# The fourth feed-forward's gate and upper half: seven half-size products in place of eight for sixteen of its 22 column tiles

## The chip, the cores and the metric

The kernel runs on one core of a Trainium2 chip. The metric is the device time of one launch in microseconds; the median of three timed runs is compared. A second kind of run is profiled: one execution of the program recorded by the hardware profiler, from which all rows below come.

## The reference

The model is a two-layer backbone with four feed-forward blocks (FFNs). The change concerns the last of them. All tensors are float32; there are 512 tokens, the model width is 1024 and the hidden width `D_FF` is 2816.

```
def swiglu(h, w_gu, w_down):
    g, u = jnp.split(h @ w_gu, 2, axis=-1)
    return (jax.nn.silu(g) * u) @ w_down
...
x = x + 0.5 * m[8] * swiglu(modulate(x, m[6], m[7]), ffn_w_gu[l, 1], ffn_w_down[l, 1])
```

`modulate` is an RMS norm with a scale and a shift. Behind the last FFN there is only a final RMS norm, and the output.

## The kernel before

Activations lie transposed: 128 rows of the width on the partitions, tokens along the free axis. `h` is a list of 8 such blocks of 128 x 512 (`KD` = 8). The hidden width is cut into 22 column tiles `j` of 128 (`NJ` = 22). For a tile, `wgu(j)` loads two weights of 128 x 1024 float32 (gate and upper, 512 KB each, by SyncE's DMA queue), and `gu_x(j, w, FULL)` multiplies each with `h`.

Float32 accuracy is had from a rounded format (`F32R`) by splitting. Every operand is a pair: `hi`, the rounded value, and `lo`, the rest. ScalarE (ACT) makes `hi` by a cast, VectorE (DVE) makes `lo` by a subtraction (`load_w`, lines 162 and 164). `mm3` (lines 169 to 171) then issues three matmuls for each block: hi·hi, lo·hi, hi·lo. A tile so has 2 x 8 x 3 = 48 matmuls of 512 columns into two PSUM banks `g` and `u`. `evac` (lines 356 to 360) empties them: ACT's Silu, DVE's product, ACT's cast (`ah`) and DVE's rest (`al`).

`ffn` works the 22 tiles in four chunks of 6, 6, 6 and 4. After each of the first three, `down` multiplies the finished tiles with the down weights: 8 output blocks `m`, each 6 x 3 matmuls of 512 columns into a bank `dps`, and a residual into `x` on DVE (line 272). After the fourth chunk `down_tails` does the same for one half of the tokens and then the other (`SEG`), with weights kept from `tail_w`. Tiles 0 and 1 are computed first, by `gu_first`, and tile 21 in two halves of the tokens beside the tail.

A scheduler puts the traced instructions into one fixed order for each engine and adds the semaphores; on the chip each engine works its own list strictly in that order. Buffers come from pools: 3 each of `raw`, `wh` and `wl` (128 x 1024), 56 slots of 128 x 512, 6 temporaries; PSUM has 4 single banks and 2 pairs of banks.

Of the kernel before, what the change touches and what calls it, by code (L numbers as in the profile page):

```python
# [11 lines left out]
F32 = mybir.dt.float32  # L12
# [7 lines left out]
P = 128  # L20
# [16 lines left out]
DOWN_AT = (0, 0, 0, 0, 0)  # L37

FOLD_AT = 8
IDLE = (5, 8)  # L40
ADA0 = dict(early=4, late=4, first_down=2, down=1, ctx=1)
ADA1 = dict(begin=2, end=20, a=2.2, b=3)
# [6 lines left out]
def kernel(ctx, tc, a):  # L49
# [56 lines left out]
    @contextmanager  # L106
    def behind(last):

        with ExitStack() as st:
            for i in last or ():  # L110
                st.enter_context(tc.issue_after(i))
            yield
# [3 lines left out]
    def bank(name):  # L116

        if fill_in:
            return fill_in[0]
        return singles.tile([P, 512], F32, tag="ps", name=nm(name))  # L120
# [43 lines left out]
            nc.vector.tensor_tensor(wl, raw, wh.bitcast(F32), ALU.subtract)  # L164
        return wh, wl

    def mm3(ps, w, x, first, last):

        nc.tensor.matmul(ps, w[0], x[0], start=first, stop=False)  # L169
        nc.tensor.matmul(ps, w[1], x[0], start=False, stop=False)  # L170
        nc.tensor.matmul(ps, w[0], x[1], start=False, stop=last)  # L171

    def rsqrt(v, w, eps=EPS, mk=None):

# [96 lines left out]
    def residual(ps, xt, gt):  # L271
        nc.vector.scalar_tensor_tensor(xt, ps, gt, xt, ALU.mult, ALU.add)  # L272

    def down(wsrc, k0, nk, outs, hook=None):

        for m in range(KD):
            w = load_w(wsrc(m, k0, nk), [P, nk, P])
            for xt, yt, gt, wd in outs:
                ps = bank("dps")[:, :wd]
                for i in range(nk):  # L280
                    mm3(ps, (w[0][:, i], w[1][:, i]), yt(k0 + i), i == 0, i == nk - 1)
                residual(ps, xt(m), gt(m))
            if hook is not None:
                hook(m)

    def tail_w(wsrc, k0, nk):
        return [load_w(wsrc(m, k0, nk), [P, nk, P], True) for m in range(KD)]

    calls = [0]

    def down_tails(ws, k0, nk, tails, first=None):

# [54 lines left out]
    def ffn(l, i, h, gate, tails, chunks, mid=None, ctx=None, extra=None, start=None, w1=None, ahead=None, between=None):  # L347

        li = 2 * l + i
        acts, actc = {}, {}

        def evac(g, u, wd, hi, lo):
            s = temp([P, wd], F32, nm("sil"))
            nc.scalar.activation(s, g, AF.Silu)  # L356
            p = temp([P, wd], F32, nm("prod"))
            nc.vector.tensor_tensor(p, s, u, ALU.mult)  # L358
            nc.scalar.copy(hi, p)  # L359
            nc.vector.tensor_tensor(lo, p, hi.bitcast(F32), ALU.subtract)  # L360

        def act_tiles(j):
            if j not in acts:
                acts[j] = (slot([P, T], F32R, nm("ah")), slot([P, T], F32R, nm("al")))
            return acts[j]

        def gu_x(j, w, sg, hook=None):
            wd = sg.stop - sg.start
            g = bank("g")[:, :wd]
            u = bank("u")[:, :wd]  # L370
            for o, ww in ((g, w[0]), (u, w[1])):
                for k in range(KD):
                    mm3(o, ww(k), hview(h[k], sg), k == 0, k == KD - 1)
                    if hook is not None and o is u and k == NORM_AT:
                        hook()
            hi, lo = act_tiles(j)
            evac(g, u, wd, hi[:, sg], lo[:, sg])

        pins = []

        def at_mid(mid, k):
            if k == MOD_AT:
                mid[0]()
                mid[1]()
                pins.extend(mark())

        def gu_first(nj, sg, weights, before=None, after=None):

            wd = sg.stop - sg.start
            if wd == T:  # L390
                o = [bank("gu") for _ in range(4)] + [t[:, b] for t in (banks("gu"), banks("gu")) for b in range(2)]
            else:
                o = halves(2 * nj, "gu")
            for k in range(KD):
                if before is not None:
                    before(k)
                w = weights(k)
                for i, ps in enumerate(o):
                    mm3(ps, w(i), hview(h[k], sg), *(ends(i, k, KD) if wd < T else (k == 0, k == KD - 1)))
                if after is not None:  # L400
                    after(k)
            for j in range(nj):
                hi, lo = act_tiles(j)
                evac(o[2 * j], o[2 * j + 1], wd, hi[:, sg], lo[:, sg])

        def gu_c(j, w, hook=None):
            b = bank("gc").rearrange("p (a t) -> p a t", a=2)
            for i, ww in enumerate(w):
                for k in range(KD):
                    mm3(b[:, i], ww(k), hcv(k), k == 0, k == KD - 1)  # L410
                    if hook is not None and i == 1 and k == NORM_AT:
                        hook()
            t = slot([P, 2, TC], F32R, nm("ac"))
            actc[j] = t
            evac(b[:, 0], b[:, 1], TC, t[:, 0], t[:, 1])

        def wgu(j):
            out = []
            for q in range(2):
                w = load_w(a["wgu"][li, j, q], [P, KD, P])  # L420
                out.append(lambda k, w=w: (w[0][:, k], w[1][:, k]))
            return out

        def wsrc(m, k0, nk):
            return a["wdn"][li, m][:, k0:k0 + nk]

        def hcv(k):
            return ctx["h"][k][:, 0], ctx["h"][k][:, 1]

        def yc(k):  # L430
            return actc[k][:, 0], actc[k][:, 1]

        if start is not None:
            gu_first(4, FULL, *start)
            j1 = 4
        else:
            def weights(k):
                return lambda i: w1[i](k)

            gu_first(2, SEG[0], weights, after=lambda k: at_mid(mid, k))  # L440
            gu_first(2, SEG[1], weights)
            j1 = 2
        last = len(chunks) - 1
        for ci, (c0, cn) in enumerate(chunks):
            if ci == last:
                with behind(mark(DVE, ACT, SP) if li == 0 else None):
                    ws = tail_w(wsrc, c0, cn)
            for j in range(max(j1, c0), c0 + cn):
                with behind(pins if j < 4 else None):
                    w = wgu(j)  # L450
                if j == NJ - 1:
                    if ctx is not None:
                        gu_c(j, w)
                    gu_x(j, w, SEG[0])
                    first = [None] * (len(tails) - 1) + [partial(gu_x, j, w, SEG[1])]
                    if between is not None:
                        first.append(between)
                else:
                    gu_x(j, w, FULL)
                    if ctx is not None and ci > 0:  # L460
                        gu_c(j, w)
                    first = None
                if j == NJ - 3:
                    wn = ahead()
                if extra is not None:
                    extra(j)
            if ci < last:
                outs = [(lambda m: xs[m], lambda k: acts[k], gate, T)]
                if ctx is not None and ci > 0:
                    outs.append((cx, yc, ctx["gate"], TC))  # L470
                down(wsrc, c0, cn, outs, hook=None if extra is None else lambda m: extra(ci, m))
            if ctx is not None and ci == 1:

                for b0, bn in chunks[:1]:
                    for j in range(b0, b0 + bn):
                        gu_c(j, wgu(j))
                        extra(-1)
                    down(wsrc, b0, bn, [(cx, yc, ctx["gate"], TC)])
        tl = []
        for kind, aft in tails:  # L480
            if kind == "ctx":
                tl.append((cx, yc, ctx["gate"], TC, aft))
            else:
                tl.append((lambda m, sg=kind: xs[m][:, sg], lambda k, sg=kind: hview(acts[k], sg), gate,
                           kind.stop - kind.start, aft))
        return down_tails(ws, *chunks[-1], tl, first), wn
# [583 lines left out]

    st3 = ExitStack()
    apool = st3.enter_context(tc.tile_pool(name="apool1", bufs=2))
    ymix = yb + ya
    h3, tails = next_h(0, 6, SEG)

# [71 lines left out]
    st3.close()  # L1147
    st4 = ExitStack()
    fpool = st4.enter_context(tc.tile_pool(name="fpool", bufs=1))
    wnh = fpool.tile([P, D], F32R, name="wnh")  # L1150
    wnl = fpool.tile([P, D], F32R, name="wnl")

# [292 lines left out]
```

## Time and profile before

| | |
|---|---|
| three timed runs | 1996.32 us median (1995.39 to 1997.0) |
| the profiled execution | 2007.54 us, of which the span from first to last instruction is 2005.8 us |
| TensorE (PE) busy | 98% of the span |
| DVE, ACT, GpSimd (POOL) busy | 60%, 35%, 1% |
| mean granted TensorE clock | 0.996 of full speed |
| the fourth FFN | about 1632 to 1990 us of the span |

A row of a group of instructions gives line, engine, operation, output and inputs with shapes, count, busy time, mean time of one, and the idle time before them. A row of the timeline gives start, duration, engine, line and operation. Records of instructions that follow each other on one engine overlap a little, since the next starts before the last has ended.

### The profile page before, as it was taken

To read this page: it belongs to the slowest core of one execution; us is meant where nothing else is said; L and a number is where in the kernel's file an instruction comes from. 1 tells how busy PE (TensorE), PEld (TensorE's weight loads), DVE (VectorE), ACT (ScalarE), POOL (GpSimd) and SP (SyncE) were. 2 spreads that over 40 slices of the span, in tenths; PEclk is the share of its full clock that TensorE was granted. 3 is DMA by queue.
4 is the path that set the end of the run, shared out by engine and by line. 5 is a ranking of instruction groups with operands and counts; after the bars stand their busy time and mean duration, and the time that the engine had idled before them with its cause. 6 is when DMAs were issued, how large, how long until landed. Compare 5 with 4: busy or idle time off the path is not lost.

```text
span 2005.8 us, 27095 instructions
## 1 busy us (share of the span) xinstructions
PE 1968.6 (98%) x10687; PEld 1704.3 (85%) x10687; DVE 1194.8 (60%) x2160; ACT 706.0 (35%) x1161; POOL 22.3 (1%) x49
## 2 busy tenths in 40 slices
PE   7999999999999999999999999999999999999998
PEld 5878899888998877988888898887878998888887
DVE  7984567466386569845555565566673673334344
ACT  4332224212264257632222343232333642222324
POOL 0000000000000110000000000000000000000000
PEclk9999999999999999999999999999999999999999
DMA  8773346456213632244545533568673142323331
GB/s 293 255 240 116 103 150 223 155 182 215 84 43 111 170 109 64 75 149 135 186 140 178 171 113 107 170 210 274 221 267 121 61 147 83 110 82 108 105 100 43
DMA packets 96742, 294.31 MB, mean 147 GB/s; under 512 B 11717, under 2 KB 15077, under 8 KB 96614
## 3 DMA queue, kind: packets, MB, share of 16 engines
q1 hardware_dynamic: 94950, 288.37, 44.5%
q0 software_dynamic: 1664, 4.20, 0.8%
q8 instruction: 84, 1.38, 0.3%
q14 instruction: 44, 0.36, 0.1%
HBM read 270.50 MB, written 11.53 MB: 141 GB/s over the span
## 4 chain that ended last, share of the span: by engine, by line
PE 85%; DVE 6%; DMA 5%; ACT 2%; issue 1%; SPq 0%; DVEq 0%; ACTq 0%
PE dps L171 9%; PE dps L169 9%; PE dps L170 9%; PE g L169 6%; PE g L170 6%; PE g L171 6%; PE u L169 6%; PE u L170 6%; PE u L171 6%; DMA aw<-in_adaT 3%; PE gc L171 2%; PE gc L170 2%; PE gc L169 2%; DVE junk L240 2%; PE gu L169 1%; PE pj L169 1%
## 5 line engine op out<-in xcount | busy, mean ns | idle before, releaser
L162 ACT CAST wh<-raw 128x1024 fp32r<-128x1024 f32 (+3 forms) x309 | 299.1, 969 | 593.8 <-PE dps L171 257.3
L164 DVE TENSOR_TENSOR wl<-raw,wh 128x1024 fp32r<-128x1024 f32 (+3 forms) x309 | 346.8, 1124 | 258.5 <-ACT wh L162 255.9
L169 PE MATMUL u<-hh,wh 128*128 128x512 f32 (+1 forms) x656 | 249.3, 380 | 0.0
L170 PE MATMUL g<-hh,wl 128*128 128x512 f32 (+1 forms) x656 | 248.9, 379 | 0.0
L169 PE MATMUL g<-hh,wh 128*128 128x512 f32 (+1 forms) x656 | 248.9, 379 | 0.0
L171 PE MATMUL u<-hl,wh 128*128 128x512 f32 (+1 forms) x656 | 248.7, 379 | 0.0
L171 PE MATMUL g<-hl,wh 128*128 128x512 f32 (+1 forms) x656 | 248.7, 379 | 0.0
L170 PE MATMUL u<-hh,wl 128*128 128x512 f32 (+1 forms) x656 | 248.7, 379 | 0.0
L169 PE MATMUL dps<-ah,wh 128*128 128x512 f32 x576 | 226.9, 394 | 6.3 <-ACT ah L359 6.3
L171 PE MATMUL dps<-al,wh 128*128 128x512 f32 x576 | 226.3, 393 | 1.2 <-DVE al L360 1.2
L170 PE MATMUL dps<-ah,wl 128*128 128x512 f32 x576 | 226.3, 393 | 0.0
L272 DVE SCALAR_TENSOR_TENSOR x<-dps,modx,x 128x512 f32<-128x512 f32 (+1 forms) x176 | 106.6, 624 | 142.0 <-PE dps L171 141.6
L240 DVE SCALAR_TENSOR_TENSOR junk<-aw,cb 128x1024 bf16<-128x1024 f32 x144 | 175.4, 1218 | 21.3 <-DMA aw<-in_adaT 21.3
L358 DVE TENSOR_TENSOR prod<-sil,u 128x512 f32<-128x512 f32 (+1 forms) x82 | 54.0, 658 | 180.6 <-PE u L171 178.3
L171 PEld LDWEIGHTS g<-hl,wh 128*128 128x128 f32 x656 | 123.5, 188 | 23.1
L171 PEld LDWEIGHTS u<-hl,wh 128*128 128x128 f32 x656 | 123.5, 188 | 23.0
L169 PEld LDWEIGHTS u<-hh,wh 128*128 128x128 f32 x656 | 123.5, 188 | 23.1
L170 PEld LDWEIGHTS u<-hh,wl 128*128 128x128 f32 x656 | 123.4, 188 | 23.1
L169 PEld LDWEIGHTS g<-hh,wh 128*128 128x128 f32 x656 | 123.5, 188 | 22.8
L170 PEld LDWEIGHTS g<-hh,wl 128*128 128x128 f32 x656 | 123.6, 188 | 22.6
L356 ACT ACTIVATE sil<-g 128x512 f32<-128x512 f32 (+1 forms) x82 | 47.3, 577 | 265.9 <-PE g L171 265.9
L169 PEld LDWEIGHTS dps<-ah,wh 128*128 128x128 f32 x576 | 109.3, 190 | 29.7 <-ACT ah L359 7.5
(355 smaller groups left out, 3693.7 us busy)
## 6 DMA issues: line engine op xcount, KB each, us to landing
raw<-in_wgu SPq DMA_DIRECT2D x172, 512.0 KB, 3.6
aw<-in_adaT SPq DMA_DIRECT2D x160, 512.0 KB, 4.5
raw<-in_wdn SPq DMA_DIRECT2D x72, 384.0 KB, 3.1
raw<-in_wdn SPq DMA_DIRECT2D x16, 512.0 KB, 3.6
rk<-in_wdn SPq DMA_DIRECT2D x32, 256.0 KB, 3.8
rk<-in_wgu SPq DMA_DIRECT2D x24, 256.0 KB, 3.7
raw<-in_wdn SPq DMA_DIRECT2D x16, 320.0 KB, 2.9
wfd<-fr SPq DMA_DIRECT2D x9, 512.0 KB, 2.9
```

The costliest lines, as they stand in the source:

```text
L162: nc.scalar.copy(wh, raw)
L164: nc.vector.tensor_tensor(wl, raw, wh.bitcast(F32), ALU.subtract)
L169: nc.tensor.matmul(ps, w[0], x[0], start=first, stop=False)
L170: nc.tensor.matmul(ps, w[1], x[0], start=False, stop=False)
L171: nc.tensor.matmul(ps, w[0], x[1], start=False, stop=last)
L240: nc.vector.scalar_tensor_tensor(junk, w, 1.0, c, ALU.mult, ALU.mult, accum_out=out)
L272: nc.vector.scalar_tensor_tensor(xt, ps, gt, xt, ALU.mult, ALU.add)
L356: nc.scalar.activation(s, g, AF.Silu)
L358: nc.vector.tensor_tensor(p, s, u, ALU.mult)
```

## The change

The fourth FFN's tiles 5 to 20 are computed in another way (`SEVEN = {3: 5}`: FFN number 3, from tile 5). Gate and upper of a tile are seen as a 2 x 2 block product: two weights by two halves of the width, times two halves of the width by two halves of the tokens (`A` = 0 to 255, `B` = 256 to 511). That is eight products of 4 blocks by 256 tokens; Strassen's method, in Winograd's form, does it in seven. The names of the products are those of their weight operand: A11 and A12 (gate, first and second half of the width), A22 (upper, second half), and four sums S1 to S4 of the weights' quarters. Each product is 4 x 3 matmuls of 256 columns.

- `combine`, once, behind `gu_first`: the four sums of `h`'s quarters for the moving side (`tk`). POOL rebuilds the eight float32 blocks and makes half of the sums; DVE makes the other half and the rests, ACT the casts.
- `seven_w(j)`, for each tile: the same two loads of 512 KB as before; the four sums of the weights on POOL (four `tensor_tensor` of 128 x 512), then hi and lo of seven quarter-tiles on ACT and DVE. `s23`, which holds S2 and S3, has one buffer.
- `seven(j, w)`: the products, in the order A11, A12, (S4 of the tile before), S2, S3, (A22 of the tile before), S1. A11, S2, S1 and S4 add to one PSUM bank `p`, of which ACT takes a copy after each of the first three; A12 goes to a bank `q` beside it (tile `sg` holds both), S3 and A22 to a bank `r` (PSUM tile `su`). DVE adds what is copied to what comes later. `plus` and `less` are DVE's `scalar_tensor_tensor`.
- `down(..., amid=...)`: the last tile of a chunk has its S4 and A22 done inside the first output block; the last of the six steps of blocks 0 and 1 is put off until block 1's other steps are done.
- The tail's kept weights are loaded in two halves, the second one at tile 21.

```
+SEVEN = {3: 5}
...
+        if amid is not None:
+            (xt, yt, gt, wd), = outs
+            tiles = []
+            for m in range(2):
+                w = load_w(wsrc(m, k0, nk), [P, nk, P])
+                ps = bank("dps")[:, :wd]
+                for i in range(nk - 1):
+                    mm3(ps, (w[0][:, i], w[1][:, i]), yt(k0 + i), i == 0, False)
+                if m == 0:
+                    amid()
+                tiles.append((w, ps))
...
+        def less(out, x, y):
+            nc.vector.scalar_tensor_tensor(out, x, 1.0, y.bitcast(F32), ALU.mult, ALU.subtract)
...
+        def combine():
+            for k in range(KD // 2):
+                f = []
+                for q in (k, k + KD // 2):
+                    t = slot([P, T], F32, nm("hf"))
+                    nc.gpsimd.tensor_tensor(t, h[q][0].bitcast(F32), h[q][1].bitcast(F32), ALU.add)
+                    f.append(t)
...
+                nc.gpsimd.tensor_tensor(t34[:, A], f[1][:, B], f[0][:, B], ALU.subtract)
+                nc.gpsimd.tensor_tensor(t34[:, B], f[1][:, A], t12[:, B], ALU.subtract)
...
+        def seven_w(j):
+            rg, ru = (wpool.tile([P, 1024], F32, tag="raw", name=nm("raw")) for _ in range(2))
...
+            s23 = pool.tile([P, 1024], F32, tag="s23", name=nm("s23"), bufs=1)
+            s1, s4 = (slot([P, 512], F32, nm("sf")) for _ in range(2))
+            for o, x, y, op in ((s1, ru[:, H0], ru[:, H1], ALU.add), (s23[:, H0], s1, rg[:, H0], ALU.subtract),
+                                (s23[:, H1], rg[:, H0], ru[:, H0], ALU.subtract),
+                                (s4, rg[:, H1], s23[:, H0], ALU.subtract)):
+                nc.gpsimd.tensor_tensor(o, x, y, op)
...
+            def halved(x, w):
+                nc.scalar.copy(w[0], x)
+                less(w[1], x, w[0])
+            a12, s2_3 = pair(), pair()
+            halved(rg, a12)
+            halved(s23, s2_3)
+            s1_ = [slot([P, 512], F32R, nm("ws")) for _ in range(2)]
+            halved(s1, s1_)
+            s4_22 = pair()
+            halved(ru[:, H1], [t[:, H1] for t in s4_22])
+            halved(s4, [t[:, H0] for t in s4_22])
...
+        def seven(j, w):
+            def product(ps, name, new):
+                for k in range(4):
+                    mm3(ps, w[name](k), B_[name](k), k == 0 and new, k == 3, not new)
+            pg = banks("sg")
+            p, q = pg[:, 0, :256], pg[:, 1, :256]
+            s, t, u = (temp([P, T], F32, nm(n)) for n in ("sil", "st", "su"))
+            product(p, "A11", True)
+            nc.scalar.copy(s[:, A], p)
+            product(q, "A12", True)
+            plus(s[:, A], q, s[:, A])
+            nc.scalar.activation(s[:, A], s[:, A], AF.Silu)
+            if late:
+                late.pop(0)()
+            product(p, "S2", False)
+            nc.scalar.copy(t[:, A], p)
+            r = bank("su")[:, :256]
+            product(r, "S3", True)
+            if late:
+                late.pop(0)()
+            product(p, "S1", False)
+            nc.scalar.copy(t[:, B], p)
+            plus(u[:, B], r, t[:, B])
+            def gate():
+                product(p, "S4", False)
+                nc.scalar.activation(s[:, B], p, AF.Silu)
+            def upper():
+                product(r, "A22", False)
+                plus(u[:, A], r, t[:, A])
+                nc.vector.scalar_tensor_tensor(u, s, 1.0, u, ALU.mult, ALU.mult)
+                hi, lo = act_tiles(j)
+                nc.scalar.copy(hi, u)
+                less(lo, u, hi)
+            late.extend((gate, upper))
```

The scheduler mixes the products of neighbouring tiles further. Three places follow, with the buffer numbers kept. In the changed kernel `sg_2888`, `wh_2882`, `wl_2883`, `ws_2884` and `ws_2885` belong to tile 8 and `sg_2908`, `wh_2900` to tile 9; `su_2872` (on PE) is tile 7's bank `r`.

TensorE, about tile 8. Before, the gate's last matmuls and the upper's first:

```order
L169 MATMUL g_2851_16019<-hh7_2610_14536,wh_2846_16008 128x512
L170 MATMUL g_2851_16019<-hh7_2610_14536,wl_2845_16007 128x512
L171 MATMUL g_2851_16019<-hl7_2611_14537,wh_2846_16008 128x512
L169 MATMUL u_2852_16020<-hh0_2596_14522,wh_2849_16014 128x512
L170 MATMUL u_2852_16020<-hh0_2596_14522,wl_2848_16013 128x512
```

TensorE at the end of tile 8 in the changed kernel: the end of S2, the last three matmuls of A22 of tile 7, and the start of S1 (line numbers are those of the changed file).

```order
L171 MATMUL sg_2888_16120<-th_2745_15303,wh_2882_16104 128x256
L172 MATMUL sg_2888_16120<-th_2745_15303,wl_2883_16105 128x256
L173 MATMUL sg_2888_16120<-tl_2746_15304,wh_2882_16104 128x256
L171 MATMUL su_2872_16046<-th_2747_15307,wh_2866_15983 128x256
L172 MATMUL su_2872_16046<-th_2747_15307,wl_2867_15984 128x256
L173 MATMUL su_2872_16046<-tl_2748_15308,wh_2866_15983 128x256
L171 MATMUL sg_2888_16120<-th_2721_15249,ws_2884_16110 128x256
L172 MATMUL sg_2888_16120<-th_2721_15249,ws_2885_16111 128x256
```

Three matmuls now stand between the last write of S2 and the first of S1 into the same bank, which waits for ACT's copy of it.

ACT, from tile 8 to tile 9. Before, two casts of weights and one tile's `ah` and Silu take turns:

```order
L359 CAST ah_2817_15859<-prod_2820_15863 128x512
L356 ACTIVATE sil_2831_15931<-g_2827_15879 128x512
L162 CAST wh_2837_15944<-raw_2838_15945 128x1024
L162 CAST wh_2846_16008<-raw_2847_16009 128x1024
L359 CAST ah_2829_15929<-prod_2832_15933 128x512
```

ACT in the changed kernel: the copy after tile 8's S2 (line 493), tile 9's gate weights (452), tile 7's result (511), the copy after tile 8's S1 (499), tile 9's S2 and S3 (452).

```order
L493 COPY st_2890_16122<-sg_2888_16120 128x256
L452 CAST wh_2900_16233<-raw_2895_16222 128x1024
L511 CAST ah_2893_16204<-su_2871_15992 128x512
L499 COPY st_2890_16122<-sg_2888_16120 128x256
L452 CAST wh_2902_16235<-s23_2897_16226 128x1024
L452 CAST ws_2904_16241<-sf_2898_16227 128x512
L486 COPY sil_2909_16252<-sg_2908_16251 128x256
```

The copy after S1, on which S4 of tile 8 waits, stands behind a cast that waits for DVE.

DVE, tile 10 to 11. Before, one tile has two rests of weights, one product and one rest of the result:

```order
L164 TENSOR_TENSOR wl_2848_16013<-raw_2850_16015,wh_2849_16014 128x1024
L358 TENSOR_TENSOR prod_2844_16003<-sil_2843_16001,u_2840_15950 128x512
L164 TENSOR_TENSOR wl_2857_16077<-raw_2859_16079,wh_2858_16078 128x1024
L360 TENSOR_TENSOR al_2842_16000<-prod_2844_16003,ah_2841_15999 128x512
L164 TENSOR_TENSOR wl_2860_16083<-raw_2862_16085,wh_2861_16084 128x1024
```

DVE in the changed kernel, about tile 10: its sum after A12 (line 410, `sil_2929`), four of its rests (407: S2 with S3, S1, A22, S4), the sum after A22 of tile 9 (410, `su_2911`), and then the rest of tile 11's gate weights.

```order
L410 SCALAR_TENSOR_TENSOR sil_2929_16383<-sg_2928_16382,sil_2929_16383 128x256
L407 SCALAR_TENSOR_TENSOR wl_2923_16367<-s23_2917_16357,wh_2922_16366 128x1024
L407 SCALAR_TENSOR_TENSOR ws_2925_16373<-sf_2918_16358,ws_2924_16372 128x512
L407 SCALAR_TENSOR_TENSOR wl_2927_16377<-raw_2916_16354,wh_2926_16376 128x512
L407 SCALAR_TENSOR_TENSOR wl_2927_16377<-sf_2919_16359,wh_2926_16376 128x512
L410 SCALAR_TENSOR_TENSOR su_2911_16254<-su_2912_16308,st_2910_16253 128x256
L407 SCALAR_TENSOR_TENSOR wl_2941_16496<-raw_2935_16484,wh_2940_16495 128x1024
```

The rest of the next tile's gate weights, for which A11 of that tile waits, now stands behind a sum that waits for A22.

## Rows read from the trace of the kernel before

**Rows 1.** The page's head and its busy times.
```profile
span 2005.8 us, 27095 instructions
PE 1968.6 (98%) x10687; PEld 1704.3 (85%) x10687; DVE 1194.8 (60%) x2160; ACT 706.0 (35%) x1161; POOL 22.3 (1%) x49
```

**Rows 2.** Busy time by stretch: tiles 2 to 5, tiles 6 to 11.
```profile
core 0: us, PE busy (x) PEld busy (x) DVE busy (x) ACT busy (x) POOL busy (x), PEclk, DMA share, GB/s
1655.00:1699.00 44.00, 44.00 (x200) 36.62 (x199) 13.51 (x17) 11.90 (x18) 0.00 (x0) 1.00 0.26 82
...
1731.00:1797.00 66.00, 66.00 (x293) 54.67 (x292) 21.36 (x23) 17.69 (x23) 0.00 (x0) 1.00 0.31 94
```

**Rows 3.** Timeline of PE: first matmul of `u`, tiles 2 and 3.
```profile
1661.42 0.39 PE L169 MATMUL u<-hh,wh 128*128 128x512 f32 x1
...
1672.30 0.39 PE L169 MATMUL u<-hh,wh 128*128 128x512 f32 x1
```

**Rows 4.** Timeline of PE in `gu_first`, 75 matmuls of 256 columns apart.
```profile
1640.23 0.28 PE L170 MATMUL gu<-hh,ws 128*128 128x256 f32 x1
...
1649.23 0.28 PE L170 MATMUL gu<-hh,ws 128*128 128x256 f32 x1
```

**Rows 5.** Groups of DVE by shape, 1650 to 2006 us.
```profile
L164 DVE TENSOR_TENSOR wl<-raw,wh 128x1024 fp32r<-128x1024 f32 x40 | 48.9, 1225 | 76.7 <-ACT wh L162 76.7
...
L360 DVE TENSOR_TENSOR al<-prod,ah 128x512 fp32r<-128x512 f32 x19 | 13.0, 685 | 0.7 <-ACT ah L359 0.7
L272 DVE SCALAR_TENSOR_TENSOR x<-dps,modx,x 128x256 f32<-128x256 f32 x16 | 6.9, 477 | 6.5 <-PE dps L171 6.5
```

**Rows 6.** Groups of ACT by shape, 1650 to 2006 us.
```profile
L162 ACT CAST wh<-raw 128x1024 fp32r<-128x1024 f32 x39 | 40.8, 1048 | 75.0 <-issue 35.4 <-PE dps L171 27.9 <-PE u L171 11.7
...
L359 ACT CAST ah<-prod 128x512 fp32r<-128x512 f32 x19 | 11.7, 616 | 4.6 <-DVE prod L358 4.6
...
L193 ACT ACTIVATE sq<-x 128x256 f32<-128x256 f32 x16 | 5.9, 407 | 9.4 <-DVE x L272 9.3
...
L356 ACT ACTIVATE sil<-gu 128x256 f32<-128x256 f32 x2 | 0.8, 384 | 4.5 <-PE gu L171 4.5
```

**Rows 7.** Timeline of DVE, instructions that follow each other without a wait.
```profile
1473.64 1.21 DVE L1127 TENSOR_TENSOR fold<-fold,fr 128x1024 fp32r<-128x1024 f32 x1
1474.77 0.67 DVE L360 TENSOR_TENSOR al<-prod,ah 128x512 fp32r<-128x512 f32 x1
1475.38 0.67 DVE L164 TENSOR_TENSOR ws<-rk,ws 128x512 fp32r<-128x512 f32 x1
```

**Rows 8.** Timeline: hand-overs from ACT to DVE and from PE to DVE.
```profile
1667.11 1.05 ACT L162 CAST wh<-raw 128x1024 fp32r<-128x1024 f32 x1 [3.89 <-issue]
1668.06 0.62 ACT L359 CAST ah<-prod 128x512 fp32r<-128x512 f32 x1
1668.19 1.23 DVE L164 TENSOR_TENSOR wl<-raw,wh 128x1024 fp32r<-128x1024 f32 x1 [0.44 <-ACT wh L162]
...
1707.43 0.39 PE L171 MATMUL dps<-al,wh 128*128 128x512 f32 x1
...
1707.86 0.75 DVE L272 SCALAR_TENSOR_TENSOR x<-dps,modx,x 128x512 f32<-128x512 f32 x1 [2.21 <-PE dps L171]
```

**Rows 9.** Groups of POOL: all that it computes on tiles.
```profile
L1178 POOL MEMSET fnh<- 128x258 f32 x1 | 0.3, 313 | 729.6 <-DMA wfd<-fr 729.6
masks.py:199 POOL TENSOR_SCALAR_AFFINE_SELECT ident<-ident 128x128 f32<-128x128 f32 x1 | 0.3, 287 | 0.1
masks.py:197 POOL MEMSET ident<- 128x128 f32 x1 | 0.2, 204 | 0.3 <-POOLq L1433 0.3
L1433 POOL MEMSET const-float32-0.0<- 128x1 f32 x1 | 0.1, 98 | 0.2 <-issue 0.2
```

**Rows 10.** The page's group of DVE's instruction with two SBUF inputs.
```profile
L240 DVE SCALAR_TENSOR_TENSOR junk<-aw,cb 128x1024 bf16<-128x1024 f32 x144 | 175.4, 1218 | 21.3 <-DMA aw<-in_adaT 21.3
```

**Rows 11.** DMA issues from 1650 us on: count, KB, median us to landing.
```profile
raw<-in_wgu SPq DMA_DIRECT2D x37, 512.0 KB, 3.5
```

More of the change, by code (lines that the diff above doesn't have):

```diff
@@ L165, in load_w, with mm3 @@
         return wh, wl
[L167 to L171, printed above, removed]
+    def mm3(ps, w, x, first, last, more=False):
+        nc.tensor.matmul(ps, w[0], x[0], start=first, stop=False, skip_group_check=more)
+        nc.tensor.matmul(ps, w[1], x[0], start=False, stop=False, skip_group_check=more)
+        nc.tensor.matmul(ps, w[0], x[1], start=False, stop=last, skip_group_check=more)
     def rsqrt(v, w, eps=EPS, mk=None):
@@ L272, in residual, with down @@
         nc.vector.scalar_tensor_tensor(xt, ps, gt, xt, ALU.mult, ALU.add)
-    def down(wsrc, k0, nk, outs, hook=None):
-        for m in range(KD):
+    def down(wsrc, k0, nk, outs, hook=None, amid=None):
+        if amid is not None:
[9 more added lines that the diff above has]
+                tiles.append((w, ps))
+            for m, (w, ps) in enumerate(tiles):
+                mm3(ps, (w[0][:, nk - 1], w[1][:, nk - 1]), yt(k0 + nk - 1), False, True)
+                residual(ps, xt(m), gt(m))
+                if hook is not None:
+                    hook(m)
+        for m in range(0 if amid is None else 2, KD):
             w = load_w(wsrc(m, k0, nk), [P, nk, P])
@@ L284, in down, with tail_w @@
                 hook(m)
-    def tail_w(wsrc, k0, nk):
-        return [load_w(wsrc(m, k0, nk), [P, nk, P], True) for m in range(KD)]
+    def tail_w(wsrc, k0, nk, ms=range(KD)):
+        return [load_w(wsrc(m, k0, nk), [P, nk, P], True) for m in ms]
     calls = [0]
+    extra_pools = {}
     def down_tails(ws, k0, nk, tails, first=None):
@@ L352, in ffn @@
         acts, actc = {}, {}
+        extra_pool = extra_pools.get(li)
         def evac(g, u, wd, hi, lo):
@@ L377, in gu_x, with plus @@
             evac(g, u, wd, hi[:, sg], lo[:, sg])
+        tk = []
+        pool = extra_pool
+        from_j = SEVEN.get(li, NJ)
+        A, B = SEG
+        H0, H1 = slice(0, 512), slice(512, 1024)
+        def less(out, x, y):
+            nc.vector.scalar_tensor_tensor(out, x, 1.0, y.bitcast(F32), ALU.mult, ALU.subtract)
+        def plus(out, x, y):
+            nc.vector.scalar_tensor_tensor(out, x, 1.0, y, ALU.mult, ALU.add)
+        def combine():
[5 more added lines that the diff above has]
+                    f.append(t)
+                t12, t34 = (slot([P, T], F32, nm("tf")) for _ in range(2))
+                nc.vector.scalar_tensor_tensor(t12[:, A], f[0][:, B], 1.0, f[0][:, A], ALU.mult, ALU.subtract)
+                nc.vector.scalar_tensor_tensor(t12[:, B], f[1][:, B], 1.0, t12[:, A], ALU.mult, ALU.subtract)
+                nc.gpsimd.tensor_tensor(t34[:, A], f[1][:, B], f[0][:, B], ALU.subtract)
+                nc.gpsimd.tensor_tensor(t34[:, B], f[1][:, A], t12[:, B], ALU.subtract)
+                pr = []
+                for t in (t12, t34):
+                    hi = slot([P, T], F32R, nm("th"))
+                    lo = slot([P, T], F32R, nm("tl"))
+                    nc.scalar.copy(hi, t)
+                    less(lo, t, hi)
+                    pr.append((hi, lo))
+                tk.append(pr)
@@ new lines, in seven_w, with pair, half @@
+        def seven_w(j):
+            rg, ru = (wpool.tile([P, 1024], F32, tag="raw", name=nm("raw")) for _ in range(2))
+            for q, t in enumerate((rg, ru)):
+                nc.sync.dma_start(t.rearrange("p (k c) -> p k c", k=KD), a["wgu"][li, j, q])
+            s23 = pool.tile([P, 1024], F32, tag="s23", name=nm("s23"), bufs=1)
[4 more added lines that the diff above has]
+                nc.gpsimd.tensor_tensor(o, x, y, op)
+            def pair():
+                return [wpool.tile([P, 1024], F32R, tag=t, name=nm(t)) for t in ("wh", "wl")]
+            def halved(x, w):
[9 more added lines that the diff above has]
+            halved(s4, [t[:, H0] for t in s4_22])
+            def half(w, s):
+                return lambda k: tuple(t[:, s][:, k * P:k * P + P] for t in w)
+            return {"A11": half(a12, H0), "A12": half(a12, H1), "S2": half(s2_3, H0), "S3": half(s2_3, H1),
+                    "S1": half(s1_, H0), "S4": half(s4_22, H0), "A22": half(s4_22, H1)}
@@ new lines, in ffn @@
+        B_ = {"A11": lambda k: hview(h[k], A), "A12": lambda k: hview(h[k + 4], A), "S4": lambda k: hview(h[k + 4], B),
+              "S1": lambda k: hview(tk[k][0], A), "S2": lambda k: hview(tk[k][0], B),
+              "S3": lambda k: hview(tk[k][1], A), "A22": lambda k: hview(tk[k][1], B)}
+        late = []
+        def seven(j, w):
[32 more added lines that the diff above has]
+            late.extend((gate, upper))
@@ L379, in ffn, with rest_of_seven @@
+        def rest_of_seven():
+            while late:
+                late.pop(0)()
         pins = []
@@ L441, in ffn @@
             gu_first(2, SEG[1], weights)
+            if from_j < NJ:
+                combine()
             j1 = 2
@@ L446, in ffn @@
                 with behind(mark(DVE, ACT, SP) if li == 0 else None):
-                    ws = tail_w(wsrc, c0, cn)
+                    ws = tail_w(wsrc, c0, cn, range(4 if from_j < NJ else KD))
             for j in range(max(j1, c0), c0 + cn):
+                by_seven = from_j <= j < NJ - 1
                 with behind(pins if j < 4 else None):
-                    w = wgu(j)
+                    w = seven_w(j) if by_seven else wgu(j)
                 if j == NJ - 1:
@@ L453, in ffn @@
                         gu_c(j, w)
-                    gu_x(j, w, SEG[0])
+                    if from_j < NJ:
+                        ws += tail_w(wsrc, c0, cn, range(4, KD))
+                    gu_x(j, w, SEG[0], rest_of_seven)
+                    if from_j < NJ:
+                        wn = ahead()
                     first = [None] * (len(tails) - 1) + [partial(gu_x, j, w, SEG[1])]
@@ L457, in ffn @@
                         first.append(between)
+                elif by_seven:
+                    seven(j, w)
                 else:
-                    gu_x(j, w, FULL)
+                    gu_x(j, w, FULL, rest_of_seven)
                     if ctx is not None and ci > 0:
@@ L462, in ffn @@
                     first = None
-                if j == NJ - 3:
+                if j == NJ - 3 and from_j == NJ:
                     wn = ahead()
@@ L470, in ffn @@
                     outs.append((cx, yc, ctx["gate"], TC))
-                down(wsrc, c0, cn, outs, hook=None if extra is None else lambda m: extra(ci, m))
+                down(wsrc, c0, cn, outs, hook=None if extra is None else lambda m: extra(ci, m),
+                     amid=rest_of_seven if late else None)
             if ctx is not None and ci == 1:
@@ L1072 @@
     apool = st3.enter_context(tc.tile_pool(name="apool1", bufs=2))
+    extra_pools[1] = extra_pools[2] = apool
     ymix = yb + ya
```

1 line of the change is left out of this document (added).

## The prediction

> **What bounds the kernel now.** I read the page's busy times first, then busy time by stretch, then TensorE's timeline. TensorE is busy 98% of the span [rows 1]. In the stretches of the changed tiles it is busy 44.00 us of 44 and 66.00 of 66, at a granted clock of 1.00, while DVE and ACT work about a third of the time and POOL not at all [rows 2]. So the fourth FFN is as long as its list of matmuls, and only fewer columns, or a stall put between them, can change it. From the first matmul of `u` in tile 2 to that in tile 3 it is 10.88 us [rows 3]: 48 matmuls of 512 columns, 0.2267 us each. In `gu_first` 75 matmuls of 256 columns take 9.00 us, 0.1200 each [rows 4], a little more than half.
>
> **The gain.** A changed tile has 7 x 4 x 3 = 84 matmuls of 256 columns, 84 x 0.1200 = 10.08 us. Against 10.88 that saves 0.80 us a tile, 12.8 us in 16 tiles. An eighth of the columns would be 1.36; the rest goes to the dearer short matmul. This is the most the change can give.
>
> **The new work beside TensorE.** Start to start, DVE's rest of 1024 takes 1.13 us and of 512 0.61 [rows 7], recorded as 1.225 and 0.685 [rows 5]; a 256-column operation that reads PSUM records 0.477 [rows 5], some 0.40 to the next. DVE's instruction with two SBUF inputs runs at the subtraction's pace (1218 against 1225 ns) [rows 5, 10]. A changed tile gives DVE two of 1024, five of 512 and three of 256: 2.26 + 3.05 + 1.2 = 6.5 us of 10.08. ACT has two casts of 1024 (1.05), four of 512 (0.62), and five copies or Silus of 256 (about 0.40) [rows 6]: 6.6 us. POOL's sum of two tiles is not in the trace. From below, its memset grows by 109 ns from 128 to 258 columns, 0.84 ns a column, so 512 take 0.53 us. From above, `affine_select`, which reads one operand, takes 287 ns for 128 columns where the memset takes 204 [rows 9]; with 83 ns more for a second operand that is 0.37, of which 0.10 is fixed (the memset of one column), and four times the rest plus 0.10 gives 1.18. The sum reads two operands and so resembles the row that reads: I take 1.2. Four make 4.8 us a tile. The loop through the one `s23` buffer is three sums, cast and rest, 3.6 + 1.05 + 1.23 = 5.9 us, below 10.08. No engine becomes the bound by its own work.
>
> The Trainium skill's GPSIMD Engine Reference, § 3.1 Elementwise, gives 4497 ns for an add of 2048 columns on GpSimd; a quarter, 1.12 us, is an estimate by that page, and four make 4.5 us. No row of before shows such an add.
>
> The loads keep their number and size; one lands in 3.5 us [rows 11], and with three `raw` buffers POOL would have to fall about 5 us behind before one is late. `combine` puts 8 x 1.2 + 8 x 0.65 = 15 us on POOL and 8 x 0.40 + 8 x 0.61 = 8 us on DVE, beside tiles 2 to 4, 32.6 us long, where these engines have 100% and two thirds of their time free: nothing. Without that cover tile 5 would wait.
>
> **The stalls.** Seven products chain through one bank, so TensorE now waits for ACT's copies and DVE's sums where too few matmuls stand between. A 256-column matmul is done 0.16 us after the next could start (0.28 recorded, 0.12 pitch [rows 4]); a hand-over takes 0.03 to 0.04 [rows 8]. I followed the order by hand, with these prices:
>
> - Tile 8: S1 waits for the copy after S2, with three matmuls between (0.36): 0.16 + 0.03 + 0.40 + 0.03 - 0.36 = 0.26.
> - Tile 9: counting from tile 8's start, A22 of tile 7 ends at 8.64. DVE adds (from 8.84, 0.48) and multiplies (0.69 [rows 5]): 10.0. ACT then casts `ah` (0.62): 10.6, and only behind it, as ACT's order shows, copies what S1 left: 11.04. S4 of tile 8 could start at 10.46, so 0.58 is lost. S2 of tile 9 waits 0.10 for the sum after A12 (five matmuls, 0.60, against 0.16 + 0.04 + 0.48 + 0.03).
> - Tile 11: A11's second matmul needs the gate's rest, which DVE now has behind the sum after A22 of tile 9: 0.16 + 0.04 + 0.40 + 1.23 + 0.03 = 1.86, against S1 and one matmul (1.56): 0.3.
> - The same two waits as in tiles 8 and 9 (S1 behind the copy, S2 behind the sum) give 0.24 in tiles 6 and 7 together, 0.05 in tile 10.
>
> Tiles 6 to 11 so lose 1.6 us. Tiles 12 to 17 repeat the order: 1.6. Tiles 18 to 20 repeat 6 to 8: 0.5. Tile 21 has its weights' rest behind tile 19's product on DVE: about 0.3. Tile 5 starts cold: ACT casts `s23` only after the copy behind A11, DVE's rest follows the sum after A12 and ends at 4.73 from the tile's start, where the second S2 matmul could go at 3.12: 1.6. At the chunk ends the last tile's A22 is followed by 15 matmuls of 512 (3.4 us), more than sum, product, cast and rest need (2.75), so nothing. In all 5.6 us.
>
> **The sum.** -12.8 + 5.6 = -7.2 us. The profiled execution took 2007.54 us (span 2005.8 and 1.7 around it), 11.2 above the median of the three runs. The change is a difference inside a stretch where TensorE runs at 1.00 in that execution, so I subtract it from the median: 1996.3 - 7.2 = **1989.1 us**. A mean changed tile is then 10.08 + 0.35 = 10.43 us.
>
> **The rivals.** *The stalls vanish.* Copies that start sooner than I say would leave 12.8: 1983.5. For it: most of my stalls are under 0.6 us, the sum of three or four hand-overs. Against: the orders are strict, and tile 5's wait is long. *The stalls double.* If each chain costs twice what I carried, or POOL puts a sum late now and then, 11.2 of 12.8 are given back: 1994.7, no measurable change. *A shorter matmul gives nothing.* From 10.88 / 84 = 0.1295 us on, 256 columns pay nothing; the 75 in a row at 0.1200 speak against it [rows 4], and I leave this case inside the second.
>
> *DVE and POOL exclude each other* (slower). Nearly all new DVE work reads two SBUF tiles, and POOL's sums do too. If one waits while the other reads, a tile needs them in line: DVE's two-input work 2 x 1.13 + 5 x 0.61 = 5.3, POOL's 4.8, the three sums on DVE 1.2, and some 0.3 of waits for TensorE: 11.6 us a tile against 10.88 before, +0.72 x 16 = +12: 2008. It decides from a POOL sum of (10.88 - 5.3 - 1.2 - 0.3) / 4 = 1.0 us on; at the lower bound, 0.53, the tile would need 8.9 and nothing would be lost. No row of before has POOL reading a tile while DVE works [rows 2, 9], so the trace doesn't decide it. Against the full price: A11 to A22 need only parts of this chain, and buffers let the engines run ahead, so they must be at it all the time.
>
> The Trainium skill, SBUF — State Buffer, § Who interferes with whom, says that a DVE instruction with two SBUF inputs contends with a GpSimd instruction that reads SBUF, since DVE's second input comes through the read interface that they share. By that rule this rival is the mechanism to expect. With the other page's estimate of 1.12 us for a sum the tile would be 5.3 + 4.5 + 1.2 + 0.3 = 11.3 us, +0.4 x 16 = +7, some 2003 us. No run here has shown such a pair yet.
>
> **How the numbers follow.** A gain between 4 and 10 us, my forecast: 0.52. A gain over 10: 0.10. The gain eaten up, within 4.0 us: 0.15. Slower by the lock: 0.23. A measurement of this kernel tells about 0.2%, 4.0 us, from no change, so faster 0.62, same 0.15, slower 0.23. The low end takes the full gain, 1984; the high end takes in the middle of the lock's cases and leaves out some 0.12 above, 2003. My forecast's own range is 1986 to 1992.
>
> **What would show it.** Right: 84 matmuls a tile at 0.120 without gaps inside products; TensorE idle about 0.3 to 0.4 us a tile, with ACT's copy `st` and DVE's sums as releasers, and one gap of 1.6 in tile 5; tiles of 10.4; POOL sums of 0.5 to 1.2 us. Wrong: DVE's rests recorded longer than 1.23 and 0.69 while POOL works, or POOL's sums far above 1.2; TensorE waiting for `wl` or `ws` in every tile; a granted clock below 1.00 after gaps; `raw` loads late; or `combine` reaching into tile 5, with TensorE idle for microseconds there.

## The result and the profile after

The changed kernel takes 2012.09 us (median of 4 runs, 2010.53 to 2012.21) against 1996.18 before: ratio 1.0078, 95% interval 1.0060 to 1.0095. It is 15.9 us slower. The forecast was 1989.1 and the range ended at 2003.

The page's head and busy times after, beside [rows 1]:

```profile
span 2010.4 us, 28650 instructions
PE 1961.4 (98%) x11263; PEld 1719.7 (86%) x11263; DVE 1288.2 (64%) x2272; ACT 757.5 (38%) x1281; POOL 139.6 (7%) x129
```

Since the two profiled executions reach the fourth FFN at different times (`gu_first` starts at 1632.0 before and at 1621.9 after, for a reason told further below), I compare its length, from there to the end of the span: 373.8 us before, 388.5 after, +14.7. So the time is lost inside the FFN. Busy time by stretch, tiles 6 to 11 and tiles 12 to 17, beside [rows 2]:

```profile
core 0: us, PE busy (x) PEld busy (x) DVE busy (x) ACT busy (x) POOL busy (x), PEclk, DMA share, GB/s
1724.80:1795.20 70.40, 64.04 (x494) 60.71 (x493) 49.86 (x57) 34.19 (x63) 30.54 (x20) 1.00 0.28 83
1827.90:1898.40 70.50, 64.54 (x496) 61.13 (x495) 49.73 (x57) 34.19 (x63) 30.20 (x20) 1.00 0.28 84
```

Six tiles should take 6 x 10.08 = 60.5 us and take 70.4, at a granted clock of 1.00. TensorE has holes now, while DVE is busy 8.3 us a tile and not full. What ended TensorE's waits (instruction, releaser: us in all, times, longest), from 1640 us on:

```profile
PE sg L171 <- DVE sil L410: 7.3, 6, 1.4
PE sg L171 <- ACT sil L486: 4.7, 6, 1.3
PE sg L172 <- DVE wl L407: 3.3, 5, 0.9
PE u L172 <- DVE wl L166: 0.7, 1, 0.7
PE sg L171 <- ACT st L499: 0.7, 2, 0.3
```

The first row is S2 waiting for the sum behind A12; the second is A12 waiting for ACT's copy of A11; the third a product waiting for its weights' rest. This view counts only the idle time between records. By start to start of matmuls, less 0.1200 or 0.2267 each, some 26 us are lost from tile 5 to the tail, of which about 11 stand before S2 and about 8 before A12; another 1.0 is lost in tile 3 (the fourth row). The lengths agree: 388.5 - (373.8 - 12.8) = 27.5 us.

The groups of DVE and POOL by shape, from 1650 us on, beside [rows 5] and [rows 9]:

```profile
L407 DVE SCALAR_TENSOR_TENSOR wl<-sf,wh 128x512 fp32r<-128x512 f32 x16 | 24.1, 1503 | 0.0
L407 DVE SCALAR_TENSOR_TENSOR wl<-raw,wh 128x512 fp32r<-128x512 f32 x16 | 19.7, 1229 | 0.8 <-ACT wh L452 0.8
L407 DVE SCALAR_TENSOR_TENSOR al<-su,ah 128x512 fp32r<-128x512 f32 x16 | 11.0, 688 | 2.5 <-ACT ah L511 2.5
L410 DVE SCALAR_TENSOR_TENSOR su<-su,st 128x256 f32<-128x256 f32 x32 | 13.4, 419 | 24.9 <-PE su L173 24.9
...
L446 POOL TENSOR_TENSOR sf<-raw,s 128x512 f32<-128x512 f32 x16 | 28.0, 1753 | 1.0
L446 POOL TENSOR_TENSOR sf<-raw 128x512 f32<-128x512 f32 x16 | 23.4, 1461 | 118.2 <-DMA raw<-in_wgu 118.2
```

Three rows of DVE are one operation on one shape, 512 columns from two SBUF tiles: 1503, 1229 and 688 ns. Of the first two groups 12 of 16 each run beside an instruction of POOL, of the third none. How that reaches TensorE shows in tile 6's timeline (start, duration, engine, line, operation):

```profile
1727.46 1.74 POOL L446 TENSOR_TENSOR s<-raw,raw 128x512 f32<-128x512 f32 x1
1728.64 1.11 DVE L407 SCALAR_TENSOR_TENSOR wl<-raw,wh 128x512 fp32r<-128x512 f32 x1
1729.15 1.73 POOL L446 TENSOR_TENSOR sf<-raw,s 128x512 f32<-128x512 f32 x1
1729.58 0.28 PE L173 MATMUL sg<-hl,wh 128*128 128x256 f32 x1
1729.67 1.76 DVE L407 SCALAR_TENSOR_TENSOR wl<-sf,wh 128x512 fp32r<-128x512 f32 x1
1730.18 0.28 PE L173 MATMUL su<-tl,wh 128*128 128x256 f32 x1
1731.36 0.41 DVE L410 SCALAR_TENSOR_TENSOR sil<-sg,sil 128x256 f32<-128x256 f32 x1
1731.82 0.39 PE L171 MATMUL sg<-th,wh 128*128 128x256 f32 x1 [1.36 <-DVE sil L410]
```

A12 ends at 1729.86, and DVE's sum of it could start there. But DVE holds a rest that records 1.76 in place of 0.69, and the sum starts at 1731.36. With 0.61 and 0.69 for the two rests DVE would have been free at 1729.94. S2 loses 1.5 us. I had priced this wait at 0.10. The four rows of POOL and DVE also show how they hold each other up. DVE's first rest ends at 1729.75, 0.55 us behind the end of POOL's sum (1729.20); POOL's next sum ends at 1730.88, 1.1 behind that rest; and DVE's second rest ends at 1731.43, again 0.55 behind that sum. Each waits until the other's instruction is done.

### The profile page after: what moved, and what is told of

Same layout as the page of the kernel before. It is cut to its first block, busy times and chain, and to the rows that moved or that the text cites. A ratio compares the mean times of both kernels' runs of the same rounds, so it can differ in the third digit from the quotient of the medians.

```text
span 2010.4 us, 28650 instructions
## 1 busy us (share of the span) xinstructions
PE 1961.4 (98%) x11263; PEld 1719.7 (86%) x11263; DVE 1288.2 (64%) x2272; ACT 757.5 (38%) x1281; POOL 139.6 (7%) x129
## 5 line engine op out<-in xcount | busy, mean ns | idle before, releaser
L164 ACT CAST wh<-raw 128x1024 fp32r<-128x1024 f32 (+3 forms) x277 | 265.1, 960 | 487.6 <-PE dps L173 217.8
L166 DVE TENSOR_TENSOR wl<-raw,wh 128x1024 fp32r<-128x1024 f32 (+3 forms) x277 | 307.7, 1113 | 169.4 <-ACT wh L164 166.9
L171 PE MATMUL u<-hh,wh 128*128 128x512 f32 (+1 forms) x528 | 199.4, 378 | 0.1
L172 PE MATMUL u<-hh,wl 128*128 128x512 f32 (+1 forms) x528 | 198.7, 376 | 0.7 <-DVE wl L166 0.7
L171 PE MATMUL g<-hh,wh 128*128 128x512 f32 (+1 forms) x528 | 198.8, 376 | 0.0
L172 PE MATMUL g<-hh,wl 128*128 128x512 f32 (+1 forms) x528 | 198.8, 376 | 0.0
L173 PE MATMUL g<-hl,wh 128*128 128x512 f32 (+1 forms) x528 | 198.6, 376 | 0.0
L173 PE MATMUL u<-hl,wh 128*128 128x512 f32 (+1 forms) x528 | 198.6, 376 | 0.0
L173 PEld LDWEIGHTS dps<-al,wh 128*128 128x128 f32 x576 | 108.1, 188 | 24.8 <-DVE al L381 2.2
L172 PEld LDWEIGHTS dps<-ah,wl 128*128 128x128 f32 x576 | 108.2, 188 | 21.6
```

The costliest lines, as they stand in the source:

```text
L164: nc.scalar.copy(wh, raw)
L171: nc.tensor.matmul(ps, w[0], x[0], start=first, stop=False, skip_group_check=more)
L172: nc.tensor.matmul(ps, w[1], x[0], start=False, stop=False, skip_group_check=more)
L173: nc.tensor.matmul(ps, w[0], x[1], start=False, stop=last, skip_group_check=more)
```

## The experiments

All times below stand beside the kernel before on the same chip. "Length" is that of the fourth FFN from the traces, one execution each (373.8 before, 388.5 changed).

| run | timed, us | before, us | ratio (95%) | length |
|---|---|---|---|---|
| sums left out | 1995.34 | 1998.05 | 0.9981 (0.9972 to 0.9990) | 368.1 |
| q apart | 2000.54 | 1998.05 | 1.0009 (1.0000 to 1.0019) | 375.1 |
| sums on DVE | 2001.91 | 1998.05 | 1.0019 (1.0009 to 1.0030) | 375.4 |
| sums on DVE, q apart | 1997.45 | 1998.05 | 0.9993 (0.9984 to 1.0002) | 371.0 |
| idle sums | 2003.80 | 1998.48 | 1.0029 (1.0018 to 1.0039) | 379.1 |
| sums left out, q apart | 1987.08 | 1998.48 | 0.9949 (0.9937 to 0.9962) | 362.2 |
| sums on DVE, q apart, from tile 6 | 1994.11 | 1998.48 | 0.9978 (0.9968 to 0.9989) | 368.9 |
| the same, A22 behind S1 (fastest version) | 1992.76 | 1998.48 | 0.9973 (0.9962 to 0.9983) | 368.2 |
| two idle sums | 2001.84 | 1999.88 | 1.0017 (1.0004 to 1.0029) | 376.0 |
| fastest version, S4's sum on POOL | 1998.45 | 1999.88 | 0.9999 (0.9989 to 1.0009) | 372.9 |

Two theories stood at the start. **A**: DVE's instructions wait for POOL's, since both read two SBUF tiles, and DVE delivers late. **B**: `p` and `q` lie in one PSUM tile `sg`, and the scheduler tracks such a tile as a whole. So A12, which writes only `q`, waits for ACT's copy of `p`, and S2, which writes only `p`, for DVE's sum that reads `q`; the arithmetic asks for neither.

**Sums left out.**

```
-                nc.gpsimd.tensor_tensor(o, x, y, op)
...
-            halved(s23, s2_3)
+            halved(ru, s2_3)
...
-            halved(s1, s1_)
+            halved(rg[:, H1], s1_)
...
-            halved(s4, [t[:, H0] for t in s4_22])
+            halved(rg[:, H0], [t[:, H0] for t in s4_22])
```

> GpSimd's four sums of weights per tile are left out (the products S1 to S4 take plain quarters of the loaded weights, so the output is another one); everything else stays. Theory A (DVE's instructions wait for GpSimd's, both reading two SBUF tiles, and so come late for TensorE): DVE's 512-column rests all record about 0.69 us, the stalls of the 16 tiles fall from some 26 us to about 10 (the 5.6 that I carried by hand and about 0.25 a tile for A12 behind the copy of A11), and the time to 1994 to 1997. Theory B (the waits come from p and q lying in one PSUM tile, so that A12 waits for the copy of A11 and S2 for the sum after A12; contention only adds little): less than a third of the loss goes, 2005 or more.

The time is 2.7 us below before, 18.6 below the changed kernel by the two differences, as A said. DVE's groups in this run:

```profile
L407 DVE SCALAR_TENSOR_TENSOR wl<-raw,wh 128x1024 fp32r<-128x1024 f32 x32 | 39.1, 1223 | 39.1 <-ACT wh L445 39.1
L407 DVE SCALAR_TENSOR_TENSOR wl<-raw,wh 128x512 fp32r<-128x512 f32 x32 | 20.7, 687 | 2.8 <-ACT wh L445 2.7
```

All rests have their undisturbed time. The FFN is 5.7 us shorter than before, of 12.8 possible.

**q apart.**

```
-            pg = banks("sg")
-            p, q = pg[:, 0, :256], pg[:, 1, :256]
+            p, q = banks("sg")[:, 0, :256], banks("sq", "q")[:, 0, :256]
```

For the last FFN, `banks` takes single banks from a pool of two `p` and two `q`, the same four banks as the two pairs.

> A12's bank q becomes a PSUM tile of its own, so that A12 no longer waits for ACT's copy of p, nor S2 for DVE's sum that reads q; GpSimd's sums stay. Theory B: the 8.1 us before A12 and the 10.9 us before S2 go, 1993 to 1997. Theory A: DVE is late all the same, the waits move to the next thing that DVE delivers (rests for S2, A11 and S4, the copies behind them), and at most half is won: 2001 to 2007.

13.4 us are won, between the two expectations and nearer to B's. The waits behind the sum and the copy of A11 are all but gone, and others have come in their place:

```profile
PE sg L176 <- DVE wl L411: 4.0, 6, 1.2
PE sg L175 <- ACT st L496: 3.9, 3, 1.3
...
PE sg L175 <- ACT sil L489: 0.5, 1, 0.5
```

These are rests and copies that DVE and ACT deliver late. So B's waits need not be, and DVE's lateness makes them long; neither theory is all.

**Sums on DVE.**

```
-                nc.gpsimd.tensor_tensor(o, x, y, op)
+                nc.vector.tensor_tensor(o, x, y, op)
```

> The four sums of weights go from GpSimd to DVE (2.4 us more on DVE a tile, 8.9 of 10.1 in all); nothing else changes. Theory A: without GpSimd beside it every DVE instruction has its undisturbed time, 0.69 us for 512 columns; the sums come as soon as before, and the time falls to 1995 to 2000, not below the version without sums. If it is DVE's load as such and not the contention that makes it late, the time stays at 2010 or rises.

It is 3.9 us above before, 12.0 below the changed kernel: DVE has more work and is nevertheless less late. Its 512-column rests record 684 to 688 ns again. The 2 us above my range are in part ahead of the FFN, whose length is 1.6 above before.

**Sums on DVE, q apart.** Both edits.

> Both edits: sums on DVE, q in a tile of its own. If A and B each cause a part, they add: stalls of 3 to 6 us in the 16 tiles, 1986 to 1990, faster than the kernel before. If B is all, it equals the version with q apart alone; if A is all, the version with the sums on DVE alone.

The parts add in kind, but not to the size I expected: 0.6 us below before, not to be told from it. Of some 9 us that are left from tile 5 on, 3.1 are in tile 5 (its start) and 0.8 each before S4 in four tiles; the rest are waits of 0.3 us and less.

**Idle sums.** The operands are changed as in the run without sums, and POOL's four instructions stay.

> GpSimd computes its four sums as in the change, but nothing reads them: the products take plain quarters of the weights, as in the run without sums (so the output is another one). Nobody waits for GpSimd's results, only its reading beside DVE is left. If contention is the cause, most of the 18 us between the change and the run without sums come back: 2004 to 2010, DVE's 512-column rests again 1.2 us and more. If the cause is that ACT and DVE wait for late sums, the time stays at that of the run without sums, 1994 to 1998.

Just under the range for contention: 5.3 above before, 8.0 above the run without sums. Nobody reads these sums; their running beside DVE is enough:

```profile
L407 DVE SCALAR_TENSOR_TENSOR wl<-raw,wh 128x1024 fp32r<-128x1024 f32 x32 | 49.7, 1554 | 31.9 <-ACT wh L452 31.7
L407 DVE SCALAR_TENSOR_TENSOR ws<-raw,ws 128x512 fp32r<-128x512 f32 x16 | 15.4, 960 | 0.0
L410 DVE SCALAR_TENSOR_TENSOR su<-su,st 128x256 f32<-128x256 f32 x32 | 13.3, 416 | 13.9 <-PE su L173 13.4 <-ACT st L499 0.5
```

The 1024-column rest takes 1554 in place of 1223 ns. The mean of the 512-column rest, 960, is below the 1.2 us that I expected, since 10 of the 16 meet no sum of POOL and take at most 0.70. The sum that reads PSUM and one SBUF tile keeps its 416, though 21 of these 32 run beside a POOL instruction. And TensorE's waits:

```profile
PE sg L171 <- DVE sil L410: 8.5, 9, 1.0
```

Only the wait behind the sum is left. The other two of the changed kernel (4.7 behind ACT's copy, 3.3 behind DVE's rests, together 8.0) are gone: those came from sums that were read late. 15.9 - 5.3 = 10.6 us is what the late sums cost in time. This splits the 18.6 us into about 8 for DVE held up and about 10.6 for ACT and DVE waiting for POOL. The lengths give 11.0 and 9.4, so about half each is as much as can be said. The second half is not free of the first cause: POOL's sums are late also because DVE holds them up. How much of it would stay with sums of 1.29 us is not shown.

**Sums left out, q apart.**

> Sums left out (another output) and q in a tile of its own: neither GpSimd beside DVE nor the waits for the shared tile. The ceiling of the seven products with this order: losses of 1 to 3 us in the 16 tiles against 12.8 of gain, 1986 to 1989. If hand-overs of the products themselves (copies of p) cost as much as the shared tile, it stays at the run without sums, 1994.

11.4 us faster, within the expectation. Six tiles, from A11 of tile 6 on, fill their time without a hole:

```profile
1723.30:1783.80 60.50, 60.50 (x494) 59.97 (x494) 36.51 (x56) 33.89 (x62) 0.00 (x0) 1.00 0.33 107
```

Of these 494 matmuls 480 are of the seven products; they begin at 1723.35, and the next matmul behind them starts at 1780.94: 57.59 us, 0.1200 each. So the pace of the seven products is as forecast, and the whole loss of the changed kernel is waits.

**From tile 6** (sums on DVE, q apart).

```
-SEVEN = {3: 5}
+SEVEN = {3: 6}
```

> Sums on DVE, q apart, and the seven products only from tile 6: tile 5, which lost 3.1 us at its start, is done plainly and gives up 0.8 of gain. Expected 2.3 us less than the version from tile 5, 1994 to 1996. If the loss at the start belongs to the first changed tile whichever it is, it moves to tile 6 and the time does not fall, but rises by 0.8.

4.4 us faster than before; the start's loss does not move to tile 6, whose weights are made during the down matmuls.

**A22 behind S1.**

```
-            if late:
-                late.pop(0)()
             product(p, "S1", False)
             nc.scalar.copy(t[:, B], p)
             plus(u[:, B], r, t[:, B])
+            if late:
+                late.pop(0)()
```

> As the last, and A22 of the tile before is issued behind S1 rather than ahead of it, so that ACT's copy behind S1 no longer stands behind the cast of the finished tile: the 0.8 us before S4 in four tiles go, 1 to 3 us less than the last, 1991 to 1994, the fastest correct one. If DVE, 80% busy with the sums on it, is the one that is late, the waits move to S2 and nothing is won.

5.7 us faster than before, 1.3 more than the last, whose interval overlaps this one's. The wait behind ACT's copy (2.2 us in all, in four places) is gone, and a smaller one for DVE's rests has come:

```profile
PE sg L176 <- DVE wl L411: 1.9, 6, 0.4
```

Of the versions that leave no work out it is the fastest.

**Two idle sums.** Two of the four, read by nobody.

> As the run with idle sums, with two of the four sums of a tile instead of four, again read by nobody (another output). If what four idle sums cost, 8.5 us beside the run without sums, is their reading beside DVE, half of it stays: 1998 to 2001, that is 0 to +3 us beside the kernel before. If it comes from something that the first sum brings (the loaded weights kept longer, one more reader to wait for), the time stays at 2003 to 2005.

2.0 above before, within 0 to +3: none gives -2.7, two +2.0, four +5.3. By its interval, +0.8 to +5.8 us, the time alone does not exclude the second case, and by the lengths the loss does not grow in step: the first two sums cost 7.9 us, the next two 3.1. The trace says more:

```profile
L506 DVE SCALAR_TENSOR_TENSOR su<-sil,su 128x512 f32<-128x512 f32 x16 | 20.7, 1297 | 0.4
PE sg L171 <- DVE sil L410: 6.3, 9, 1.0
```

The first row is DVE's product of a tile. Nine of the 16 record 1.76 to 1.77 us beside a sum of POOL, the others 0.68 to 0.69. The rest `al` needs the product and stands ahead of DVE's sum behind A12, so S2 waits nine times. With four idle sums the same product has the same mean, 1297 ns, and `al` between is longer too, up to 1.02 us. So what a sum of POOL costs depends on which instruction of DVE it meets, and their number alone does not give it.

**S4's sum on POOL**, the rest as the fastest version.

```
-                nc.vector.tensor_tensor(o, x, y, op)
+                (nc.gpsimd if o is s4 else nc.vector).tensor_tensor(o, x, y, op)
```

> As the fastest correct version so far (sums on DVE, q apart, from tile 6, A22 behind S1), with the last sum, S4, given back to GpSimd: DVE has 0.61 us a tile less, GpSimd one sum of 1.3 to 1.7 beside it. If DVE's load is what still costs, 1 to 3 us are won, 1989 to 1992. If the reading side by side costs more than the load it takes away, as in the runs with idle sums (about 2 us for each sum), it is slower by 0 to 3, 1993 to 1996.

1.4 below before, where the fastest version is 5.7 below: one sum handed back to POOL costs some 4 us (4.7 by the lengths), more than the 0 to 3 that I expected. TensorE's waits for DVE's rests grow from 1.9 to:

```profile
PE sg L176 <- DVE wl L411: 6.2, 9, 1.3
```

## Why the prediction was wrong

- **The gain** held. The run without sums and with q apart has 0.1200 us for each matmul of the six tiles, 10.08 a tile; 11.4 of 12.8 us came out.
- **The stalls** failed, 5.6 us forecast and some 26 measured. This is the step that was wrong, and it was wrong twice. I had priced every DVE instruction at its undisturbed time from a trace in which POOL does nothing; beside POOL those of 512 columns took up to 1.79 us in place of 0.69. And of the waits that come from `p` and `q` lying in one tile I had carried S2's behind the sum, at about 0.1 us, and not A12's behind the copy of A11: giving `q` a tile of its own won 13.4 us. Tiles 6 to 11 lose 9.9 us instead of 1.6, tile 5 2.5 instead of 1.6. Where DVE is undisturbed, the sum was of the right size: the run without sums has 12.8 - 5.7 = 7.1 us of losses, one of them in tile 3. But that is luck: I had not seen that A12 waits for the copy of A11, and without the sums tile 5 has no wait for `s23`, for which I had 1.6.
- **The rival that DVE and POOL exclude each other** was the one that came. It gave 2008 and 11.6 us a tile; measured were 2012.09 and 70.4 / 6 = 11.7. Its premise holds: one waits while the other works. But its figure came so close partly by luck. It had 5.3 + 4.8 = 10.1 us of such work in line in a tile, 60.6 in six; in tiles 6 to 11 a sum of POOL or a two-input instruction of DVE runs in 53.9 of the 70.4 us, and in the other 16.5 neither does. I had asked whether that line fits into a tile, and taken from "buffers let the engines run ahead" that it rarely bites. What costs is that single instructions come 1 to 1.5 us late where TensorE stands right behind them. My high end, 2003, took the middle of this rival's cases and so cut off the one that came.
- The Trainium skill, SBUF — State Buffer, § Who interferes with whom, named this contention, and the traces agree: DVE's two-input instructions go from 0.69 to as much as 1.79 us, the one with a single SBUF input stays at 0.42. Between row and rule I had put 0.23 on the rule; no row spoke against it.
- **POOL's sum** was taken as 1.2 us, by the upper bound of 1.18; undisturbed it takes 1.29, so the upper bound was none. The Trainium skill's GPSIMD Engine Reference, § 3.1 Elementwise, led to an estimate of 1.12; the measurement decides.
- **`combine`**, costed at nothing, cost 1.0 us in tile 3, where a rest of weights stands behind it on DVE.
- **The chunk ends** cost nothing, as forecast, and the granted clock stayed at 1.00.

One thing ahead of the fourth FFN has to be kept apart. It starts at 1621.9 to 1626.3 us in the profiled executions of all these kernels and at 1632.0 in that of before, and the edits are not the reason. Up to 1364 us the executions of before and of the changed kernel are 1.0 us apart; by 1525 they are 10.7 apart. In that of before, between these times:

```profile
1368.27 1.22 DVE L240 SCALAR_TENSOR_TENSOR junk<-aw,cb 128x1024 bf16<-128x1024 f32 x1 [4.76 <-DMA aw<-in_adaT]
1369.42 0.68 DVE L358 TENSOR_TENSOR prod<-sil,u 128x512 f32<-128x512 f32 x1
1370.81 0.79 PE L169 MATMUL dps<-ah,wh 128*128 128x512 f32 x1 [2.77 <-ACT ah L359]
...
1370.10:1376.90 6.80, 6.09 (x14) 4.37 (x15) 6.04 (x12) 2.49 (x3) 0.00 (x0) 0.50 0.68 212
```

DVE waits 4.76 us for a load, the product behind it comes late, and TensorE stands still for 2.77. The last row is a stretch of busy time as above: the granted clock is 0.50, the lower of its two levels (1.2 of 2.4 GHz), for 6.8 us. At 1476, behind two waits of 1.87 and 0.81, it is 0.50 again for 3.4 us. In the changed kernel's execution TensorE waits 0.55 there and the clock stays at 1.00. In three of the ten runs, sums left out among them, it fell at about 1369, and in that with the sums on DVE at 1468. The lengths leave this stretch out and the times hold it. The 2 to 3 us by which the two differ in those two runs may come from it; the timed executions have no trace that would show it. Why the load is late in some executions stays open.

## What to carry to other kernels

When work goes to an engine that was idle, the durations of its neighbours are no longer those of the old trace: ask first whether they hold each other up when both read SBUF, as DVE and POOL do here, and let that case set the end of the range. An engine at 70% can still be late everywhere, if the waiting engine stands right behind single instructions of it; count the distance to each consumer, not the load. And two banks in one tile bind their users together: where halves are written and read apart, make them tiles apart.

## What the runs showed of the hardware

- A DVE instruction of 512 columns with two SBUF inputs takes 0.68 to 0.69 us alone and up to 1.79 beside POOL's sums; POOL's sum takes 1.28 to 1.30 alone and up to 2.17 in the changed kernel. They take turns by whole instructions: in the changed kernel, from 1675 us on, all 32 DVE instructions of 512 columns and two SBUF inputs that start while a sum of POOL runs end 0.55 us behind it, and of the 34 sums that start while such an instruction of DVE (512 or 1024 columns) runs 33 end 1.14 to 1.17 behind it.
- DVE's sum of 256 columns with one input in PSUM and one in SBUF takes 0.41 to 0.43 us, whether POOL runs or not.
- The four sums of 512 columns cost less on DVE with DVE fuller (2001.91, 3.9 above before) than on POOL with DVE emptier (2012.09, 15.9 above).
